# Modulation blocks laid out contiguous, a pinned order for the opening, and the convolution's taps split around the attention

## The chip, the cores and the metric

The kernel runs on one core of a Trainium2 chip: five engines with a queue each (TensorE or PE for matmuls, VectorE or DVE, ScalarE or ACT, GpSimd or POOL, SyncE or SP, which here only issues DMAs), an on-chip memory SBUF, and PSUM, into which TensorE writes. The metric is the device time of one execution in microseconds, as a median over runs.

## What is computed

One layer of a hybrid block on 512 tokens of width 1024, all in float32. Cut to what matters here:

```python
mod = silu(c) @ mod_w + mod_b                    # c: 1024 values; mod_w: 1024 x 6144
sh1, sc1, g1, sh2, sc2, g2 = split(mod, 6)
h = rms_norm(x, norm1_g) * (1 + sc1) + sh1       # x: 512 x 1024
proj = h @ w_in                                  # w_in: 1024 x 7680, split into ten parts
cv_a, cv_g, hg_q, hg_f, hg_i, hg_g, sb_q, sb_k, sb_v, gl = split(proj, ...)
u = causal_conv31(cv_a * sigmoid(cv_g)) + b      # 512 channels, 31 taps each
y_conv = silu(layer_norm(u)) @ w_conv            # branch 1
y_hgrn = gated_linear_recurrence(hg_q, hg_f, hg_i, hg_g) @ w_hgrn    # branch 2
y_sb = stick_breaking_attention(sb_q, sb_k, sb_v) @ w_sb             # branch 3, 8 heads
x = x + g1 * ((sig(gl0) * y_conv + sig(gl1) * y_hgrn + sig(gl2) * y_sb) @ w_out)
x = x + g2 * (relu(mod_norm(x) @ w1) ** 2 @ w2)
```

## The kernel before, in words

Activations lie transposed, 128 channels on the partitions and 512 tokens along the row. Each operand of a large matmul is split into a rounded part and the rest (`hilo`: ACT writes the rounded part at L83, DVE subtracts at L84), and each product is three matmuls (`mm3`, L113 to L115). Weights are loaded by SP in pieces of 1 MB (`cols_stage`, L329) and split in the order in which `add_cols` and `add_rows` list them, two pieces ahead of their use.

The program is written in one order, and a scheduler fixes each engine's own order from that and from its model of durations; an instruction that is ready may be taken ahead of earlier ones. An engine then runs its list strictly in that order. `tc.issue_after(i)` adds a rule: what is traced inside it stands behind instruction `i` on `i`'s engine. `high_priority` moves work ahead.

**Opening.** Small vectors (`vecs`) and the tap weights (`conv_w`) come on ACT's queue; x (four tiles), then the modulation block and the 768 weight columns of slab 0 on SP's. A modulation block (`load_ms`) is the part of `mod_w` that gives shift and scale for 128 channels: two DMAs of 512 KB in pieces of 512 B. PE first transposes vectors and tap weights (L170, L175), runs eight warm-up matmuls (L285), and then goes through eight slabs. For slab j: `prep_mod` multiplies the block by silu(c) into two accumulators, adds them on DVE (L241), and sums over partitions on PE with a vector of ones (L245); `prep_h` transposes x (L254), modulates (L258) and splits it; `prep_w` splits the slab's weights; `first_mm` makes 18 matmuls into six PSUM banks: two tiles of `cv_a` and the four of `cv_g`. Before slab 0, `x_norm` squares (ACT) and scales (DVE, L226) each x tile.

**After it.** Four tiles `k_in`, four `q_in` (24 matmuls each), the scans of `decay` (L616), `scores` (whose first product per head pair is `gram`, L650), the rows `hv_in` and `states`; then two more `cv_a` tiles (`conv_in`), eight `sb_in` tiles and `sv_in` for the attention; then four head pairs of attention, with a gate tile `hg_in` after each. A head's part of it is three score matmuls per row block, two sigmoids on ACT, a reversed running product and a product on DVE (L545, L546), transposes on PE (L557) and the product with v (L573).

**Taps.** The convolution is 31 DVE instructions for each of four channel tiles, `tap(i, d)`. The first of each is traced behind `head_norm`; the other 120 wait in a list and are traced within the branches at the end (`hook0`, `hook1`), with the attention ahead of them in program order. `conv_sum` and `conv_norm` follow them, and branch `cv`, the last of three, needs their result.

Of the kernel before, what the change touches and what calls it, by code (L numbers as in the profile page):

```python
# [15 lines left out]
P = 128  # L16
# [22 lines left out]
def tile_hybrid_block(ctx, tc, x, vecs, mod_w, mod_b, w_in, conv_w, w_conv, w_hgrn, w_sb, w_out, w1, w2, out):  # L39
# [42 lines left out]
    def hilo(src, hi, lo):  # L82
        A.activation(hi, src, AF.Copy)  # L83
        V.tensor_tensor(out=lo, in0=src, in1=hi.bitcast(F32), op=ALU.subtract)  # L84
# [25 lines left out]
    def mm3(o, lhs, rhs, start, stop):  # L110
        lh, ll = lhs
        rh, rl = rhs
        TE.matmul(o, lhsT=lh, rhs=rh, start=start, stop=False)  # L113
        TE.matmul(o, lhsT=lh, rhs=rl, start=False, stop=False)  # L114
        TE.matmul(o, lhsT=ll, rhs=rh, start=False, stop=stop)  # L115
# [3 lines left out]
    A.dma_start(vrow, vecs)  # L119
    cw_row = S((CW, 512), g="c0")  # L120
    A.dma_start(cw_row, conv_w)
# [13 lines left out]
    slabs = {}  # L135

    def load_slab(j):
        slabs[j] = wpool.tile([P, W0], F32, name="slab", bufs=10)
        SY.dma_start(slabs[j], wi_row[:, j, C_A + 256:C_A + 256 + W0])

    for t in range(NT):
        xt.append(P4((P, D), g="x0"))
        SY.dma_start(xt[t], x_v[t])
    load_ms(0)
# [28 lines left out]
    cp = ax()  # L173
    for i in range(4):
        TE.transpose(cp[:, i * 32:i * 32 + CW], cw_row[:, i * P:(i + 1) * P], ident[0:CW, 0:CW])  # L175
    cwc = C([P, 4, 32], F32)
    V.tensor_copy(cwc[:, :, 0:CW], cp[:, 0:128].rearrange("p (i k) -> p i k", k=32)[:, :, 0:CW])

# [18 lines left out]

    gbh = C([P, 24], F32)
    V.tensor_scalar(out=gbh, in0=vcol[:, V_GB:V_GB + 24], scalar1=0.5, scalar2=None, op0=ALU.mult)
    lnh = C([P, 8], F32)  # L200
    V.tensor_scalar(out=lnh, in0=vcol[:, V_LG:V_LG + 8], scalar1=0.5, scalar2=None, op0=ALU.mult)
# [9 lines left out]

    facc = [mm() if i < 4 else ps("f") for i in range(6)]
    hT, fw = [], {}
# [8 lines left out]
    def x_norm(t):  # L222
        junk = P4((P, D), g="x0")
        after(first, junk, xt[t], AF.Square, accum_out=stat[:, t:t + 1])
        rstd_small(stat[:, 4 + t:5 + t], stat[:, t:t + 1], D)
        V.tensor_scalar(out=xt[t], in0=xt[t], scalar1=stat[:, 4 + t:5 + t], scalar2=None, op0=ALU.mult)  # L226

    def prep_mod(j):
        ms = ms_t.pop(j)
        acc = S((P, 2, 2, P), g="acc")  # L230
        for kk in range(KT):
            a, src, c = acc[:, kk % 2], ms[:, :, kk, :], cact[:, kk:kk + 1]
            if kk < 2 and j == 0:
                V.tensor_scalar(out=a, in0=src, scalar1=c, scalar2=None, op0=ALU.mult)
            elif kk < 2:
                A.activation(a, src, AF.Identity, scale=c)
            else:
                V.scalar_tensor_tensor(out=a, in0=src, scalar=c, in1=a, op0=ALU.mult, op1=ALU.add)
        ne = 2 if j == 0 else 1
        if ne == 1:  # L240
            V.tensor_tensor(out=acc[:, 0], in0=acc[:, 0], in1=acc[:, 1], op=ALU.add)  # L241
        tp = ps("tp")
        for q in range(2):
            for e in range(ne):
                TE.matmul(tp[:, q:q + 1], lhsT=acc[:, e, q, :], rhs=ones[:, 0:1], start=(e == 0), stop=(e == ne - 1))  # L245
        gs, sh = modc[:, j:j + 1], modc[:, 8 + j:9 + j]
        V.scalar_tensor_tensor(out=gs, in0=tp[:, 0:1], scalar=mb1[:, j:j + 1], in1=vcol[:, V_N1 + j:V_N1 + j + 1], op0=ALU.add, op1=ALU.mult)
        V.tensor_tensor(out=sh, in0=tp[:, 1:2], in1=vcol[:, V_MB + j:V_MB + j + 1], op=ALU.add)

    def prep_h(j):  # L250
# [7 lines left out]
        b = A.activation(hf, tq, AF.Identity, scale=gs, bias=sh)  # L258
        if j == 3:
            ph.ops.append(b)  # L260
        hilo(hf, hh, hl)
        hT.append((hh, hl))

# [5 lines left out]
    def prep(j):  # L269
        load_ms(j)  # L270
        load_slab(j)
        prep_mod(j)
        prep_h(j)
        prep_w(j)

    def first_mm(j):
        wh, wl = fw.pop(j)
        for i in range(6):
            c = slice(i * P, (i + 1) * P)
            mm3(facc[i], (wh[:, c], wl[:, c]), hT[j], j == 0, j == KT - 1)  # L280
# [245 lines left out]

    LAY = {0: (0, 0), 1: (1, 0), 3: (1, 384), 2: (2, 0)}
    FILL = (512, 512, 256)

    def sb_weights(h):  # L530
# [3 lines left out]
        for tb in range(NT):  # L534
# [11 lines left out]
            V.tensor_tensor(out=bt[:, 0:n - 1], in0=bt[:, 0:n - 1], in1=kp[:, 1:n], op=ALU.mult)  # L546
# [249 lines left out]
    hnh = C([P, 1], F32)  # L796
    V.tensor_scalar(out=hnh, in0=vcol[:, V_HN:V_HN + 1], scalar1=0.5, scalar2=None, op0=ALU.mult)
# [16 lines left out]
    for i in range(2):  # L814
        conv_in(i, ch_tile("ca", i))
    for i in range(4):
# [98 lines left out]

    def hook0(j):
        run_bg(5, taps)
# [3 lines left out]
    def hook1(j):  # L921
        for d, f in ((0, lambda: (run_bg(len(taps), taps), conv_sum())), (1, conv_center), (2, conv_norm), (3, lambda: hls.append(parts(cacc)))):
# [123 lines left out]
def host_layout(inputs):  # L1046
# [31 lines left out]
```

## Time and profile before

| | |
|---|---|
| median of 3 runs | 922.64 us (922.06 to 924.39) |
| profiled execution, its own time | 924.09 us |
| its span, first to last instruction | 922.3 us |
| PE busy | 894.8 us, 97% of the span |
| DVE busy | 599.5 us, 65% |
| ACT busy | 385.8 us, 42% |
| moved by DMA | 107.78 MB, 117 GB/s on average |

Engines work side by side, so shares do not add up. An idle engine matters only where it is the one that the others wait for; over most of this span that is PE.

### The profile page before, as it was taken

The page shows a single profiled execution, that of the slowest core. Times are in us where ns is not written, and L with a number is a line of the kernel's source. Part 1 is how long each engine was busy: PE and PEld are TensorE (multiplying, and loading weights), DVE is VectorE, ACT ScalarE, POOL GpSimd, SP SyncE. Part 2 cuts the span into 40 slices and gives each one's busy share as a digit, 9 for nine tenths or more (in the row PEclk, how much of TensorE's full clock was granted, in tenths as well). Part 3 has the DMA queues.
Part 4 walks back from the last instruction along what each step waited for, and adds up shares of the span by engine and source line. Part 5 has one row for each costly group of instructions (what it writes and reads, how often), then busy time and mean ns, then how long its engine had stood idle before and what let it go on. Part 6 is the DMA issues. An engine that isn't in the chain of part 4 may idle for free.

```text
span 922.3 us, 10624 instructions
## 1 busy us (share of the span) xinstructions
PE 894.8 (97%) x4185; PEld 728.8 (79%) x4185; DVE 599.5 (65%) x886; ACT 385.8 (42%) x596; POOL 28.1 (3%) x35
## 2 busy tenths in 40 slices
PE   4999989999988999999999999999999999999998
PEld 2788878888755588888888888888888888888886
DVE  4882388899999999997965544774423254442422
ACT  4652434475788632223833536453312123431210
POOL 1002000001032000000000000000000000000000
PEclk9999999999999999999999999999999999999999
DMA  9981301131200344793423620552242233142121
GB/s 279 279 268 59 113 12 46 52 132 46 91 1 1 115 159 162 245 329 136 138 86 103 216 70 1 192 196 91 92 137 92 56 113 106 46 137 92 68 69 46
DMA packets 85418, 107.78 MB, mean 117 GB/s; under 512 B 2270, under 2 KB 58705, under 8 KB 85368
## 3 DMA queue, kind: packets, MB, share of 16 engines
q1 hardware_dynamic: 85200, 106.96, 35.5%
q8 instruction: 33, 0.54, 0.3%
q14 instruction: 17, 0.14, 0.1%
q10 hardware_dynamic: 168, 0.14, 0.0%
HBM read 105.00 MB, written 2.10 MB: 116 GB/s over the span
## 4 chain that ended last, share of the span: by engine, by line
PE 88%; DVE 6%; ACT 3%; DMA 2%; issue 1%; SPq 1%; DVEq 0%; ACTq 0%
PE mm L113 14%; PE mm L114 14%; PE mm L115 14%; PE ax L115 9%; PE ax L113 9%; PE ax L114 9%; PE o L115 2%; PE o L114 2%; PE o L113 2%; PE g L113 2%; PE g L114 2%; PE g L115 2%; PE g L654 1%; DVE bt L545 1%; PE o L573 1%; DVE bt L546 1%
## 5 line engine op out<-in xcount | busy, mean ns | idle before, releaser
L84 DVE TENSOR_TENSOR wl<-w,wh 128x1024 fp32r<-128x1024 f32 x134 | 162.8, 1221 | 194.4 <-ACT wh L83 147.4
L83 ACT ACTIVATE wh<-w 128x1024 fp32r<-128x1024 f32 x134 | 139.8, 1054 | 290.8 <-PE ax L115 129.9
L113 PE MATMUL mm<-ht,wh 128*128 128x512 f32 x272 | 106.7, 392 | 0.0
L115 PE MATMUL mm<-ht,wl 128*128 128x512 f32 x272 | 106.6, 392 | 0.0
L114 PE MATMUL mm<-ht,wh 128*128 128x512 f32 x272 | 106.6, 392 | 0.0
L114 PE MATMUL mm<-p,wh 128*128 128x512 f32 (+1 forms) x272 | 102.6, 378 | 0.0
L115 PE MATMUL mm<-p,wl 128*128 128x512 f32 (+1 forms) x272 | 102.4, 377 | 0.0
L113 PE MATMUL mm<-p,wh 128*128 128x512 f32 (+1 forms) x272 | 102.3, 377 | 0.0
L462 DVE SCALAR_TENSOR_TENSOR cv<-cv,cbig 128x511 f32<-128x511 f32 (+29 forms) x120 | 83.5, 733 | 0.0
L113 PEld LDWEIGHTS mm<-ht,wh 128*128 128x128 f32 x272 | 51.1, 188 | 11.2 <-issue 0.8
L114 PEld LDWEIGHTS mm<-ht,wh 128*128 128x128 f32 x272 | 51.1, 188 | 11.0 <-issue 0.6
L115 PEld LDWEIGHTS mm<-ht,wl 128*128 128x128 f32 x272 | 51.1, 188 | 10.4 <-issue 0.2
L114 PEld LDWEIGHTS mm<-p,wh 128*128 128x128 f32 x272 | 51.2, 188 | 9.4
L115 PEld LDWEIGHTS mm<-p,wl 128*128 128x128 f32 x272 | 51.2, 188 | 9.4
L113 PEld LDWEIGHTS mm<-p,wh 128*128 128x128 f32 x272 | 51.0, 188 | 9.3
L113 PE MATMUL ax<-wh,p 128*128 128x512 f32 x128 | 49.8, 389 | 0.0
L114 PE MATMUL ax<-wl,p 128*128 128x512 f32 x128 | 49.8, 389 | 0.0
L115 PE MATMUL ax<-wh,p 128*128 128x512 f32 x128 | 49.8, 389 | 0.0
L113 PE MATMUL ax<-wh,s 128*128 128x512 f32 x128 | 49.8, 389 | 0.0
L114 PE MATMUL ax<-wl,s 128*128 128x512 f32 x128 | 49.8, 389 | 0.0
L115 PE MATMUL ax<-wh,s 128*128 128x512 f32 x128 | 49.8, 389 | 0.0
L865 DVE SCALAR_TENSOR_TENSOR s<-p,cbig,s 128x512 f32<-128x512 f32 x64 | 47.1, 746 | 1.5 <-DMA p<-in_mod_w_dram 1.2
(248 smaller groups left out, 1666.8 us busy)
## 6 DMA issues: line engine op xcount, KB each, us to landing
w<-in_w_dram SPq DMA_DIRECT2D x32, 1024.0 KB, 5.7
w<-in_w_in_dram SPq DMA_DIRECT2D x27, 1024.0 KB, 5.3
p<-in_mod_w_dram SPq DMA_DIRECT2D x32, 512.0 KB, 7.4
ms<-in_mod_w_dram SPq DMA_DIRECT2D x16, 512.0 KB, 5.9
w<-in_w_out_dram SPq DMA_DIRECT2D x4, 1024.0 KB
slab<-in_w_in_dram SPq DMA_DIRECT2D x8, 384.0 KB, 4.6
x<-in_x_dram SPq DMA_DIRECT2D x4, 512.0 KB, 8.9
w<-in_w_hgrn_dram SPq DMA_DIRECT2D x2, 1024.0 KB, 4.9
```

What stands on the lines that cost most here:

```text
L83: A.activation(hi, src, AF.Copy)
L84: V.tensor_tensor(out=lo, in0=src, in1=hi.bitcast(F32), op=ALU.subtract)
L113: TE.matmul(o, lhsT=lh, rhs=rh, start=start, stop=False)
L114: TE.matmul(o, lhsT=lh, rhs=rl, start=False, stop=False)
L115: TE.matmul(o, lhsT=ll, rhs=rh, start=False, stop=stop)
L462: V.scalar_tensor_tensor(out=cacc[i][:, d:], in0=cu[i][:, 0:T - d], scalar=w, in1=cacc[i][:, d:], op0=ALU.mult, op1=ALU.add)
L545: V.tensor_tensor_scan(out=kp[:, 0:n][:, ::-1], data0=kp[:, 0:n][:, ::-1], data1=kp[:, 0:n][:, ::-1], initial=1.0, op0=ALU.mult, op1=ALU.b ...
L546: V.tensor_tensor(out=bt[:, 0:n - 1], in0=bt[:, 0:n - 1], in1=kp[:, 1:n], op=ALU.mult)
L573: TE.matmul(o[h * 64:h * 64 + 64, sb * P:T], lhsT=svt[sb][:, pr * P + h * 64:pr * P + h * 64 + 64], rhs=ahs[h][bi][:, off:off + n], start= ...
L654: TE.matmul(o[:, b * n:(b + 1) * n], lhsT=l, rhs=r, start=True, stop=True)
L865: V.scalar_tensor_tensor(out=a, in0=box["s"][:, kk, :], scalar=cact[:, 2 * k2 + kk:2 * k2 + kk + 1], in1=a, op0=ALU.mult, op1=ALU.add)
```

## The change

The first 2048 columns of `mod_w` are also laid out on the host as eight blocks in which each partition's 8 KB lie together, so `load_ms` is one DMA of 1 MB, with four buffers for three. x moves to ACT's queue, behind the vectors; the tap weights and the small columns for later stages (`lb_columns`, `conv_columns`) are traced inside the slab loop. Block 0 is summed wholly on PE (`prep_sum(0)`, 16 matmuls straight from the block), and for the other slabs PE sums the two accumulators itself (two matmuls more, no addition on DVE). Six warm-up matmuls stay of eight. In the loop, the work that prepares slab j stands behind the split of slab j-2, and its sums and transposes behind the first nine matmuls of slab j-1. The weights of later stages stand behind the last slab in SP's queue.

The two `cv_a` tiles come before the q tiles. Of the 120 taps, 24 are traced with the k tiles, 12 with the two `cv_a` tiles and 16 with the q tiles; the other 68 stand behind the last product of the attention on DVE. The diff, with returned handles, `lb_columns` and a few moved lines left out:

```diff
-    cw_row = S((CW, 512), g="c0")
-    A.dma_start(cw_row, conv_w)
...
     def load_ms(j):
-        ms_t[j] = wpool.tile([P, 2, 8, P], F32, name="ms", bufs=3)
-        for q in range(2):
-            c0 = (D if q == 0 else 0) + j * P
-            SY.dma_start(ms_t[j][:, q], mw_v[:, :, c0:c0 + P])
+        ms_t[j] = wpool.tile([P, 2, 8, P], F32, name="ms", bufs=4)
+        SY.dma_start(ms_t[j], mod_a[j])
...
+    load_ms(0)
     for t in range(NT):
         xt.append(P4((P, D), g="x0"))
-        SY.dma_start(xt[t], x_v[t])
-    load_ms(0)
+        with tc.issue_after(vdma.ins):
+            A.dma_start(xt[t], x_v[t])
     load_slab(0)
...
+    def conv_columns():
+        cw_row = S((CW, 512), g="c0")
+        with tc.issue_after(hb[3].ins):
+            A.dma_start(cw_row, conv_w)
+        cp = ax()
+        for i in range(4):
+            TE.transpose(cp[:, i * 32:i * 32 + CW], cw_row[:, i * P:(i + 1) * P], ident[0:CW, 0:CW])
...
-            if kk < 2 and j == 0:
-                V.tensor_scalar(out=a, in0=src, scalar1=c, scalar2=None, op0=ALU.mult)
-            elif kk < 2:
+            if kk < 2:
                 A.activation(a, src, AF.Identity, scale=c)
...
-        ne = 2 if j == 0 else 1
-        if ne == 1:
-            V.tensor_tensor(out=acc[:, 0], in0=acc[:, 0], in1=acc[:, 1], op=ALU.add)
+        return acc
+
+    def prep_sum(j, acc=None):
         tp = ps("tp")
+        ms = None if acc is not None else ms_t.pop(j)
         for q in range(2):
-            for e in range(ne):
-                TE.matmul(tp[:, q:q + 1], lhsT=acc[:, e, q, :], rhs=ones[:, 0:1], start=(e == 0), stop=(e == ne - 1))
+            if ms is not None:
+                for kk in range(KT):
+                    TE.matmul(tp[:, q:q + 1], lhsT=ms[:, q, kk, :], rhs=cact[:, kk:kk + 1], start=(kk == 0), stop=(kk == KT - 1))
+                continue
+            for e in range(2):
+                TE.matmul(tp[:, q:q + 1], lhsT=acc[:, e, q, :], rhs=ones[:, 0:1], start=(e == 0), stop=(e == 1))
...
-    for i in range(8):
+    for i in range(6):
         TE.matmul(wu, lhsT=ident, rhs=scanm.rearrange("p a t -> p (a t)"), start=True, stop=True)
+    prep_sum(0)
     for t in range(NT):
-        x_norm(t)
-    prep_mod(0)
-    prep_h(0)
-    prep_w(0)
+        last = x_norm(t)
+    with tc.issue_after(last[0].ins), tc.issue_after(last[1].ins):
+        prep_w(0)
+    ready = [prep_h(0)]
     for j in range(1, KT + 1):
         if j < KT:
-            prep(j)
-        first_mm(j - 1)
+            load_ms(j)
+            load_slab(j)
+            behind = ready[max(j - 2, 0)]
+            with tc.issue_after(behind[0].ins), tc.issue_after(behind[1].ins):
+                acc = prep_mod(j)
+                prep_w(j)
+        mid = first_mm(j - 1, range(3))
+        if j < KT:
+            with tc.issue_after(mid.ins):
+                prep_sum(j, acc)
+                ready.append(prep_h(j))
+        first_mm(j - 1, range(3, 6))
+        if j == 2:
+            lb_columns()
+        if j == 4:
+            conv_columns()
...
-        SY.dma_start(t, wv)
+        with tc.issue_after(last_load[0].ins):
+            SY.dma_start(t, wv)
...
     add_cols("hf", w_in, H_F, 4)
+    add_cols("ca", w_in, C_A, 2)
     add_cols("hq", w_in, H_Q, 4)
     add_rows("hi", w_in, H_I, 0, KT)
-    add_cols("ca", w_in, C_A, 2)
...
-            V.tensor_tensor(out=bt[:, 0:n - 1], in0=bt[:, 0:n - 1], in1=kp[:, 1:n], op=ALU.mult)
+            sb_last[:] = [V.tensor_tensor(out=bt[:, 0:n - 1], in0=bt[:, 0:n - 1], in1=kp[:, 1:n], op=ALU.mult)]
...
-    for h in range(4):
-        k_in(h)
+    for i in (2, 3):
+        tap(i, 0)
+    for j in range(1, CW):
+        for i in (2, 3):
+            bg.append(lambda i=i, j=j: tap(i, j))
+    with tc.issue_after(mid.ins):
+        for h in range(4):
+            k_in(h)
+            run_bg(6)
+    for i in range(2):
+        conv_in(i, ch_tile("ca", i))
+        tap(i, 0)
+        run_bg(6)
+    for j in range(1, CW):
+        for i in (0, 1):
+            bg.append(lambda i=i, j=j: tap(i, j))
     HP[0] = 2000
     for h in range(4):
         q_in(h)
+        run_bg(4)
...
-    for i in range(2):
-        conv_in(i, ch_tile("ca", i))
-    for i in range(4):
-        tap(i, 0)
-    for pr in ((2, 3), (0, 1)):
-        for j in range(1, CW):
-            for i in pr:
-                bg.append(lambda i=i, j=j: tap(i, j))
...
+    def late_taps(n):
+        with tc.issue_after(sb_last[0].ins):
+            run_bg(n, taps)
+
     def hook0(j):
-        run_bg(5, taps)
+        late_taps(5)
```

## Rows read from the trace of the kernel before

**Rows 1.** Busy time in stretches: PE, PEld, DVE, ACT, POOL; clock, DMA share, GB/s.

```profile
66.00:110.00 44.00, 44.00 (x196) 36.43 (x195) 13.23 (x18) 12.45 (x17) 5.55 (x2) 1.00 0.25 82
250.00:313.30 63.30, 57.44 (x297) 38.23 (x295) 62.25 (x102) 51.24 (x117) 12.38 (x8) 1.00 0.10 34
320.00:440.00 120.00, 120.00 (x546) 99.85 (x546) 110.76 (x160) 34.99 (x44) 1.06 (x2) 1.00 0.61 214
```

**Rows 2.** Timeline of the opening: start, duration, instruction, idle time before and releaser.

```profile
10.91 0.63 PE L175 MATMUL ax<-crs,c 31*128 31x31 f32 x4 [5.71 <-DMA c<-in_conv_w_dram]
11.47 8.56 PE L285 MATMUL tq<-cbig,crs 128*128 128x512 f32 x16
...
16.27 1.04 ACT L88 ACTIVATE x<-x 128x1024 f32<-128x1024 f32 x1
17.31 0.42 ACT L88 ACTIVATE cbig<-cbig 128x1 f32<-128x1 f32 x2
...
19.88 0.95 PE L245 MATMUL tp<-crs,acc 128*128 128x1 f32 x8
20.87 0.74 DVE L226 TENSOR_SCALAR x<-x,cbig 128x1024 f32<-128x1024 f32 x1
...
22.71 0.78 ACT L258 ACTIVATE s<-tq,cbig 128x512 f32<-128x512 f32 x1 [2.04 <-DVE cbig L248]
23.98 0.51 ACT L236 ACTIVATE acc<-ms,cbig 128x256 f32<-128x256 f32 x1 [0.49 <-DMA ms<-in_mod_w_dram]
24.40 0.61 ACT L83 ACTIVATE ht<-s 128x512 fp32r<-128x512 f32 x1
...
25.06 2.07 PE L113 MATMUL mm<-ht,fwh 128*128 128x512 f32 x4 [2.63 <-ACT ht L83]
...
65.79 0.39 PE L115 MATMUL f<-ht,fwl 128*128 128x512 f32 x1
```

**Rows 3.** Busy time in short stretches of the opening; the last two columns are DMA.

```profile
0.00:2.00 2.00, 0.00 (x0) 0.00 (x0) 0.00 (x0) 0.40 (x1) 1.47 (x8) 1.00 0.12 27
...
4.00:8.00 4.00, 0.42 (x1) 0.18 (x1) 0.28 (x1) 1.25 (x3) 0.44 (x3) 1.00 1.00 369
40.00:45.00 5.00, 5.00 (x27) 4.22 (x26) 4.66 (x13) 4.20 (x7) 0.00 (x0) 1.00 1.12 325
```

**Rows 4.** Timeline of PE: first and last of 48 matmuls, then the stop.

```profile
109.31 0.39 PE L113 MATMUL ax<-wh,ht 128*128 128x512 f32 x1
...
119.96 0.39 PE L115 MATMUL ax<-wh,ht 128*128 128x512 f32 x1
122.67 0.65 PE L650 MATMUL g<-tl 128*64 128x64 f32 x8 [2.32 <-DVE tl L677]
```

**Rows 5.** The chain of waits within the slabs: start, time on the chain, what.

```profile
32.90 0.39 PE tp L245 x4
...
36.38 0.44 PE tq L254 x4
```

**Rows 6.** Timeline of slab 2: start of its summing, rounding of its tile.

```profile
32.73 0.56 PE L245 MATMUL tp<-crs,acc 128*128 128x1 f32 x4
...
34.54 0.63 ACT L83 ACTIVATE ht<-s 128x512 fp32r<-128x512 f32 x1
```

**Rows 7.** Timeline of DVE: the scans, and seven taps in a row.

```profile
113.22 4.57 DVE L616 TENSOR_TENSOR_SCAN B<-cbig,B 128x512 f32<-128x512 f32 x4 [1.62 <-ACT B L88]
...
412.64 4.53 DVE L462 SCALAR_TENSOR_TENSOR cv<-cv,cbig 128x486 f32<-128x486 f32 x7
```

**Rows 8.** Busy time of the taps' line alone (DVE) in three stretches.

```profile
190.00:250.00 60.00, 29.31 (x42) 1.00 0.16 54
250.00:313.30 63.30, 6.55 (x9) 1.00 0.10 34
313.30:440.00 126.70, 47.65 (x70) 1.00 0.59 206
```

**Rows 9.** Groups of PE from 250 to 313.3 us: busy, mean; idle before, releasers.

```profile
L557 PE MATMUL tb<-crs,bt 128*128 128x128 f32 x73 | 14.6, 281 | 4.7 <-DVE bt L546 4.1 <-ACT wh L83 0.6
```

More of the change, by code (lines that the diff above doesn't have):

```diff
@@ L38, in tile_hybrid_block @@
 @with_exitstack
-def tile_hybrid_block(ctx, tc, x, vecs, mod_w, mod_b, w_in, conv_w, w_conv, w_hgrn, w_sb, w_out, w1, w2, out):
+def tile_hybrid_block(ctx, tc, x, vecs, mod_a, mod_w, mod_b, w_in, conv_w, w_conv, w_hgrn, w_sb, w_out, w1, w2, out):
     nc = tc.nc
@@ L82, in hilo @@
     def hilo(src, hi, lo):
-        A.activation(hi, src, AF.Copy)
-        V.tensor_tensor(out=lo, in0=src, in1=hi.bitcast(F32), op=ALU.subtract)
+        a = A.activation(hi, src, AF.Copy)
+        return a, V.tensor_tensor(out=lo, in0=src, in1=hi.bitcast(F32), op=ALU.subtract)
     def after(bi, *args, **kw):
@@ L114, in mm3 @@
         TE.matmul(o, lhsT=lh, rhs=rl, start=False, stop=False)
-        TE.matmul(o, lhsT=ll, rhs=rh, start=False, stop=stop)
+        return TE.matmul(o, lhsT=ll, rhs=rh, start=False, stop=stop)
     vrow = S((NVEC, P), g="c0")
-    A.dma_start(vrow, vecs)
-    cw_row = S((CW, 512), g="c0")
-    A.dma_start(cw_row, conv_w)
+    vdma = A.dma_start(vrow, vecs)
     x_v = x.rearrange("(a p) d -> a p d", p=P)
@@ L209, in tile_hybrid_block, with lb_columns @@
     modc = C([P, 16], F32)
+    cwc = C([P, 4, 32], F32)
+    oml = C([P, 4], F32)
+    gbh = C([P, 24], F32)
+    lnh = C([P, 8], F32)
+    hnh = C([P, 1], F32)
+    def conv_columns():
[5 more added lines that the diff above has]
+            TE.transpose(cp[:, i * 32:i * 32 + CW], cw_row[:, i * P:(i + 1) * P], ident[0:CW, 0:CW])
+        V.tensor_copy(cwc[:, :, 0:CW], cp[:, 0:128].rearrange("p (i k) -> p i k", k=32)[:, :, 0:CW])
+    def lb_columns():
+        lb = vcol[:, V_HLB:V_HLB + 4]
+        lbe = C([P, 4], F32)
+        lbs = C([P, 4], F32)
+        V.tensor_tensor(out=lbe, in0=lb, in1=lb, op=ALU.subtract)
+        ph(lbe, lbe, AF.Exp)
+        V.reciprocal(out=lbs, in_=lbe)
+        V.tensor_tensor(out=lbe, in0=lbe, in1=lbs, op=ALU.mult)
+        V.tensor_tensor(out=lbs, in0=lbe, in1=lbe, op=ALU.subtract)
+        V.tensor_scalar(out=oml, in0=lbs, scalar1=-1.0, scalar2=1.0, op0=ALU.mult, op1=ALU.add)
+        V.tensor_scalar(out=gbh, in0=vcol[:, V_GB:V_GB + 24], scalar1=0.5, scalar2=None, op0=ALU.mult)
+        V.tensor_scalar(out=lnh, in0=vcol[:, V_LG:V_LG + 8], scalar1=0.5, scalar2=None, op0=ALU.mult)
+        V.tensor_scalar(out=hnh, in0=vcol[:, V_HN:V_HN + 1], scalar1=0.5, scalar2=None, op0=ALU.mult)
     facc = [mm() if i < 4 else ps("f") for i in range(6)]
-    hT, fw = [], {}
+    hT, fw, hb = [], {}, []
     def rstd_small(dst, ssq, n):
@@ L225, in x_norm @@
         rstd_small(stat[:, 4 + t:5 + t], stat[:, t:t + 1], D)
-        V.tensor_scalar(out=xt[t], in0=xt[t], scalar1=stat[:, 4 + t:5 + t], scalar2=None, op0=ALU.mult)
+        b = V.tensor_scalar(out=xt[t], in0=xt[t], scalar1=stat[:, 4 + t:5 + t], scalar2=None, op0=ALU.mult)
+        return ph.ops[-1], b
     def prep_mod(j):
@@ L267, in prep_w, with first_mm @@
         fw[j] = (wh, wl)
[L269 to L278, printed above, removed]
+    def first_mm(j, tiles):
+        wh, wl = fw[j]
+        for i in tiles:
             c = slice(i * P, (i + 1) * P)
-            mm3(facc[i], (wh[:, c], wl[:, c]), hT[j], j == 0, j == KT - 1)
+            b = mm3(facc[i], (wh[:, c], wl[:, c]), hT[j], j == 0, j == KT - 1)
+        return b
     wu = ps("tq")
-    for i in range(8):
+    for i in range(6):
         TE.matmul(wu, lhsT=ident, rhs=scanm.rearrange("p a t -> p (a t)"), start=True, stop=True)
+    prep_sum(0)
     for t in range(NT):
-        x_norm(t)
-    prep_mod(0)
-    prep_h(0)
-    prep_w(0)
+        last = x_norm(t)
+    with tc.issue_after(last[0].ins), tc.issue_after(last[1].ins):
+        prep_w(0)
+    ready = [prep_h(0)]
     for j in range(1, KT + 1):
         if j < KT:
-            prep(j)
-        first_mm(j - 1)
+            load_ms(j)
[14 more added lines that the diff above has]
+            conv_columns()
     dij = S((P, P), I32, g="mk")
@@ L921, in hook1 @@
     def hook1(j):
-        for d, f in ((0, lambda: (run_bg(len(taps), taps), conv_sum())), (1, conv_center), (2, conv_norm), (3, lambda: hls.append(parts(cacc)))):
+        for d, f in ((0, lambda: (late_taps(len(taps)), conv_sum())), (1, conv_center), (2, conv_norm), (3, lambda: hls.append(parts(cacc)))):
             if j == 4 + d:
```

32 lines of the change are left out of this document (7 added, 25 removed).

## The prediction

> **What bounds the kernel now.** I read the busy times by stretch first, then the opening in order of time, then the chain of waits. From 320 us to 440 us TensorE (PE) is busy all the time, and so it is from 66 to 110 [rows 1]; the table above says 97% for the whole span. So the only time to win lies where PE waits or does work that nobody needs: the opening, one stop near 122 us, and the attention, where PE is busy for 57.4 of 63.3 us [rows 1]. The rest can only move as a block.
>
> In the opening the reader should see three late things [rows 2]. TensorE stands 5.71 us until 10.91, because the transposes of the tap weights wait for their own DMA; the warm-up matmuls stand in line behind them and end only at 20.0. The last x tile is scaled on VectorE (DVE) from 20.87 to 21.6. Then ScalarE (ACT) waits 0.49 us for a modulation block that a later slab needs, and works on it 0.5 us, ahead of the rounding that the first real matmul waits for. That matmul starts at 25.06, and the last of slab 7 at 65.79.
>
> **The opening after the change.** The tap weights leave the front, so the warm-up starts when the vectors are in, near 5.3 us. Sixteen records took 8.56 us [rows 2]; if the first four go at half the pace of the others, as 0.86 and 0.43 us, twelve take 6.9, until 12.2. Block 0 of the modulation is then summed on PE alone: 16 matmuls, two records each, where 8 records took 0.95 us [rows 2], so 3.8 us, until 16.0. Both end before the last x tile is normalised (below, 16.6), so I cost them at nothing; if the summing ran at half the clock it would end at 19.8 and the first matmul would slip by 3 us.
>
> The last x tile sets the start. Before, x had the DMA engines nearly to itself and moved at 369 GB/s from 4 to 8 us, with hardly a byte before 2.0 us [rows 3]. Now it goes out on ACT's queue while SP sends block 0, slab 0, block 1 and so on. x is 2.1 MB. Lower bound: x as if alone, 2.0 + 2.1/0.369 = 7.7 us. Upper bound: behind all that SP can issue before it waits for a buffer (four blocks of 1.05 MB and four slabs of 0.39 MB, 5.8 MB): 2.0 + 7.9/0.369 = 23.4. I take equal shares, 4.2 MB, 13.4 us, and my allowance of 0.8 for the last bytes and the signal: 14.2. Two queues that always have work, and no row that favours one, are the reason. From there by rows 2: square to the end of its two small activations 1.46 (16.27 to 17.73), scaling 0.74, one tile of transposes 0.3, modulating 0.78, rounding 0.61, and 0.3 of gaps: 4.2. First matmul at 18.4, 6.7 us earlier than before.
>
> The Trainium skill ("DMA: Bandwidth & Descriptors", section "Queues, rings and completion order") says that each DMA engine takes turns between the queues that have work for it, one packet at a time. A second queue then gives x no bandwidth of its own: by that rule x lands at 14.2 and the sum is as above, while a reader who took the ACT queue for a private road would get 8.5 and a first matmul near 13 as far as x decides. No row here has two busy queues at once, so this case's trace does not decide it yet.
>
> **What the slabs cost after that.** Back to back a 512-column matmul takes (119.96 - 109.31)/47 = 0.2266 us [rows 4], so 144 of them take 32.6. Before, each later slab added one set of transposes, 0.44, and one summing of four records, 0.39 [rows 5]: 7 x 0.83 = 5.8. From 25.06 to 66.02 are 40.96 us; with two early matmuls of the next stage (0.45) that leaves 2.1 us for the slow clock at the start. After, the accumulators are no longer added on DVE but on PE, so a summing has eight records, 0.78: 7 x 1.22 = 8.5. This is a price of 2.7 us on the bound engine.
>
> The pinned order puts the summing in the middle of a slab's 18 matmuls. From its end to the end of the rounding took 35.17 - 32.73 - 0.39 = 2.05 us [rows 6]; transposes and nine matmuls cover 0.44 + 2.04 = 2.48. So 0.4 us to spare, which one DVE or ACT instruction in the way can use up. I put 1.5 us of stalls on seven slabs, most of it at slab 1, whose sums may start only after slab 0 is split; the bounds are 0 and 5 (0.7 each). The transfers hold nothing up: in 8 KB rows I give the modulation blocks the 369 GB/s of x, against 325 for the old mix [rows 3]; 1.44 MB per slab takes 3.9 us against a pace of 5.3 on PE. All 13.6 MB up to the last slab are due near 40 us, so the weights queued behind it have over 15 us before the stage that needs them.
>
> End of the stage: 18.4 + 32.6 + 8.5 + 2.1 + 1.5 = 63.1, against 66.02 - 0.45 = 65.6 before. **Term 1: -2.5 us.** Ends: x as if alone and no stalls would give -9.7 by this sum, but the 32 summing records (until 16.0, then modulating and rounding: 18) hold it at -4.4; x behind everything gives +7.5.
>
> **Taps before the attention.** 52 of the 120 taps go into the stretch of the k, conv and q tiles (24 + 12 + 16). Seven taps took 4.53 us in a row [rows 7], 0.647 each: 33.6 us, and 2.2 for the four first taps. DVE was busy for 13.23 of 44 us there [rows 1], so 30.8 are free; the two conv tiles now moved in add 10.9 us of PE time and, at the same share, 7.6 free. 35.8 of work in 38.4 of room: it fits, at a cost of nothing, but with 2.6 us in hand. The conv tiles only change places with later tiles; PE has them to do either way. The stop of 2.32 us at 122.67, where the first gram waits for DVE [rows 4], stays: **term 2: 0**, from -2.3 to the rival below.
>
> **Taps in and after the attention.** Before, 29.3 us of taps ran from 190 to 250, 6.6 in the attention and 47.7 after it [rows 8]. The first were free, since PE was full. Without the 6.6, DVE has 62.25 - 6.55 = 55.7 us of its own there [rows 1] and PE 57.4: PE would be the bound, so 63.3 - 57.4 = 5.9 us is the most to win. The least is nothing: an idle PE may come from the order of short steps on three engines rather than from taps. Of the 4.7 us that PE idles before the transposes, 4.1 end with the product that DVE writes [rows 9], and taps stand in that queue; I take the middle. **Term 3: -3.0 us.** Afterwards 68 taps remain, 68 x 0.70 = 47.6 us, the same as the 47.7 that ran there before, so the convolution's end keeps its distance to the attention's end and PE stays full.
>
> **Sum.** -2.5 + 0 - 3.0 = -5.5. The profiled execution took 924.09 us with a span of 922.3; so a span near 916.8, and 918.6 for such an execution. The profiled one lies 1.45 above the median of 922.64, so the prediction for the median is 917.1. About 0.3% (2.8 us) is what a measurement of this kernel can tell from no change.
>
> **Rivals.**
> 1. *x comes late.* SP's blocks have rows twice as long as those of x; if the engines' turns are counted in rows, x gets a third: 6.3 MB, 2.0 + 17.1 + 0.8 = 19.9, first matmul at 24.1, stage end 68.8, +3.2 in place of -2.5. Total 922.64 + 3.2 - 3.0 = 922.8, no change. For it: x loses the head start that it had. Against: nothing in the trace weighs queues.
> 2. *Taps hold up the scans: slower.* The 16 taps of the q tiles stand in program order ahead of the scans that the grams need. DVE has 2.6 us in hand. If they all run late, the scans (which before waited 1.62 us for ACT, [rows 7]) start 16 x 0.647 - 1.6 = 8.7 us later, and PE, already stopped there, stops as much longer: 917.1 + 8.7 = 925.8. It decides from 5.5 us of lateness, which cancels the rest, and is a measurable loss from 8.3 on. For it: 0.70 us, a tap's full length, in place of 0.647 fills the room to the last microsecond. Against: tiles of q carry only four taps, so DVE catches up there.
> 3. *All of it comes.* First matmul at 18 without stalls (-4.4), PE full in the attention (-5.9), and half of the stop at 122 gone (-1.2): 911.1. For it: DVE's own work falls below PE's in the attention. Against: every one of the three must come.
> 4. *The opening gives nothing.* If slabs stall 0.7 us each, term 1 is +0.9 and only the attention is left: 920.5.
>
> **Chances.** The forecast (-5.5, its own range 914 to 920) 0.42; rival 1 0.13; rival 2 0.15; rival 3 0.20; rival 4 0.10. The forecast gives 0.37 faster and 0.05 same; rival 3 0.20 faster; rival 4 0.04 faster and 0.06 same; rival 1 0.08 same, 0.05 slower; rival 2 0.03 same, 0.12 slower. Together 0.61 faster, 0.22 same, 0.17 slower. The range, 910 to 925, leaves out the later half of rival 2 and a third of rival 3, together 0.14.
>
> **What would show it.** The first real matmul between 17 and 20 us (24 would be rival 1); the last of slab 7 near 63; tap instructions from 64 us on with DVE over 85% busy until 118; the wait before the first gram at 2 to 3 us (8 or more is rival 2); no tap between sv's end and the last product of the attention, and PE idle there by about 3 us in place of 5.9; PE full from then on. The prediction fails most easily through an order on PE or DVE that differs from program order: an engine that stands behind one instruction that is late.

## The result, and the profile after

The changed kernel takes 930.84 us (median of 4 runs, 929.32 to 932.26) against 922.38 for the kernel before (4 runs): a ratio of 1.0087, with a 95% interval from 1.0061 to 1.0113. It is 8.5 us slower, where 917.1 was predicted; it lies outside the range, and on the side that was given 17 in 100. The profiled execution took 932.15 us with a span of 930.4.

The opening first. The timeline of the kernel after: TensorE (PE), then ScalarE (ACT) with the four x tiles.

```profile
7.64 0.43 PE L167 MATMUL ax<-crs,c 115*128 115x115 f32 x1 [7.64 <-DMA c<-in_vecs_dram]
7.86 7.51 PE L290 MATMUL tq<-cbig,crs 128*128 128x512 f32 x12
15.21 3.63 PE L252 MATMUL tp<-cbig,ms 128*128 128x1 f32 x32
...
21.44 0.47 PE L264 MATMUL tq<-crs,x 128*128 128x128 f32 x1 [2.32 <-DVE x L232]
...
24.71 2.07 PE L113 MATMUL mm<-ht,fwh 128*128 128x512 f32 x4 [2.13 <-ACT ht L83]
...
74.14 0.39 PE L115 MATMUL f<-ht,fwl 128*128 128x512 f32 x1
```

```profile
10.36 1.06 ACT L88 ACTIVATE x<-x 128x1024 f32<-128x1024 f32 x1 [1.73 <-DMA x<-in_x_dram]
...
13.34 1.06 ACT L88 ACTIVATE x<-x 128x1024 f32<-128x1024 f32 x1 [1.45 <-DMA x<-in_x_dram]
...
16.34 1.06 ACT L88 ACTIVATE x<-x 128x1024 f32<-128x1024 f32 x1 [1.52 <-DMA x<-in_x_dram]
...
19.35 1.06 ACT L88 ACTIVATE x<-x 128x1024 f32<-128x1024 f32 x1 [1.54 <-DMA x<-in_x_dram]
```

The reader should see that ACT waits for the DMA before each of the four tiles, and that they come 3.0 us apart. PE's warm-up does start earlier, at 7.86 in place of 11.47 [rows 2], and the sums of block 0 take 3.63 us, near the 3.8 worked out; but the last x tile is there only at 19.35, so the first real matmul comes at 24.71, 0.35 us earlier than before [rows 2] and not 6.7. The last matmul of slab 7 ends at 74.37 (the next starts there), against 66.02 before. From there to the end of the span are 856.0 us, and 856.7 before, counted from 65.6. So the loss lies in the eight slabs: 49.7 us from the first matmul to the end, where 40.5 were needed before.

What PE waited for in the first 75 us of the kernel after, besides the vectors (us in total, times, longest):

```profile
PE mm L113 <- ACT ht L83: 4.0, 6, 2.1
PE tq L264 <- DVE x L232: 2.5, 2, 2.3
PE ax L198 <- DMA c<-in_conv_w_dram: 1.1, 1, 1.1
```

And the stretches of the opening (the column ahead of the last two is PE's granted clock, as a share of 2.4 GHz):

```profile
4.00:8.00 4.00, 0.36 (x2) 0.39 (x3) 0.00 (x0) 0.72 (x1) 0.44 (x3) 1.00 1.00 411
10.00:15.00 5.00, 5.00 (x10) 2.06 (x9) 1.06 (x5) 3.02 (x8) 0.00 (x0) 1.00 1.02 414
15.00:20.00 5.00, 4.12 (x35) 3.66 (x33) 1.12 (x2) 2.12 (x5) 0.00 (x0) 0.91 1.02 413
20.00:25.00 5.00, 1.24 (x3) 0.65 (x4) 2.79 (x6) 3.51 (x10) 0.00 (x0) 0.50 1.02 381
25.00:30.00 5.00, 5.00 (x17) 3.93 (x17) 3.63 (x8) 2.72 (x6) 0.00 (x0) 0.57 0.54 164
```

The bytes are not the trouble: 405 to 414 GB/s move from 4 to 20 us, more than the 369 of before [rows 3]. But the clock is at half, 1.2 GHz, from about 19 us (0.91 is the mean from 15 to 20) until nearly 30 us: slab 0's matmuls run at half pace. It falls right behind the one-column sums of block 0, which end at 18.84, and PE's thin stretch (1.24 us busy from 20 to 25) comes after the fall.

I cut the stage into parts by the starts on PE's timeline: a matmul's pace of 0.2266 us; what each transpose and sum takes; how much later than the pace a matmul starts where the row names a releaser (waits); and the excess of matmuls that run at over 0.33 us each (slow clock). The last column is the twelfth experiment below.

| us | before | predicted | after | twelfth |
|---|---|---|---|---|
| first real matmul | 25.1 | 18.4 | 24.7 | 18.7 |
| 144 matmuls, small gaps | 33.6 | 32.6 | 33.8 | 33.9 |
| slow clock | 1.4 | 2.1 | 3.1 | 3.3 |
| sums | 3.0 | 5.4 | 5.6 | 2.7 |
| transposes | 2.6 | 3.1 | 2.9 | 2.9 |
| waits (for h and conv_w) | 0 | 1.5 | 4.0 | 0.4 |
| transposes of conv_w | - | - | 0.3 | - |
| end of slab 7 | 65.6 | 63.1 | 74.4 | 61.9 |

Then the other terms. The stop before the first gram, groups of the attention from 250 to 320 us (PE, VectorE or DVE, ScalarE or ACT) and its busy times, and the taps' line alone, all of the kernel after but for the first line of the third block, which is of the kernel before from 250 to 313.3 us:

```profile
142.26 0.98 PE L672 MATMUL g<-tl 128*64 128x64 f32 x7 [2.33 <-DVE tl L699]
```

```profile
L579 PE MATMUL tb<-crs,bt 128*128 128x128 f32 x63 | 12.5, 281 | 4.8 <-DVE bt L568 3.5 <-DVE hg L659 1.2
```

```profile
L545 DVE TENSOR_TENSOR_SCAN bt<-bt 128x128 f32<-128x128 f32 (+3 forms) x32 | 25.6, 824 | 0.4 <-ACT bt L88 0.3
...
L567 DVE TENSOR_TENSOR_SCAN bt<-bt 128x128 f32<-128x128 f32 (+3 forms) x29 | 22.7, 812 | 3.9 <-ACT bt L88 3.8
...
L88 ACT ACTIVATE bt<-z 128x128 f32<-128x128 f32 (+3 forms) x59 | 21.9, 430 | 3.6 <-DVE bt L568 2.8 <-PE z L563 0.6
```

```profile
250.00:320.00 70.00, 64.72 (x329) 44.83 (x329) 59.06 (x93) 59.49 (x127) 12.55 (x8) 1.00 0.09 31
```

```profile
66.00:125.00 59.00, 34.03 (x50) 1.00 0.31 103
...
250.00:330.00 80.00, 2.67 (x4) 1.00 0.21 71
330.00:460.00 130.00, 44.14 (x65) 1.00 0.50 175
```

The stop is where it was and as long (2.33 against 2.32 us, [rows 4]). The taps ran where they were meant to: 50 of them by 125 us, none in the attention (the four counted up to 330 us start at 326.29, behind its last product), 65 after that. PE still stands 5.3 us of the 70 in the attention, and 4.8 of it before the same transposes as before [rows 9]. What changed is one step further back: DVE, freed from taps, now waits 3.9 us ahead of its scans, 3.8 of them for ACT's sigmoids, and ACT in turn waits 2.8 us ahead of these for the product on DVE.

### The profile page after: what moved, and what is told of

Read it like the earlier page. It is cut to its first block, busy times and chain, and to the rows that moved or that the text cites. A ratio compares the mean times of both kernels' runs of the same rounds, so it can differ in the third digit from the quotient of the medians.

```text
span 930.4 us, 10711 instructions
## 1 busy us (share of the span) xinstructions
PE 902.2 (97%) x4233; PEld 733.6 (79%) x4233; DVE 597.9 (64%) x871; ACT 387.5 (42%) x596; POOL 34.8 (4%) x35
## 4 chain that ended last, share of the span: by engine, by line
PE 87%; DVE 5%; ACT 3%; DMA 3%; issue 1%; ACTq 0%; DVEq 0%
PE mm L113 14%; PE mm L114 13%; PE mm L115 13%; PE ax L113 9%; PE ax L115 9%; PE ax L114 9%; PE o L114 2%; PE o L113 2%; PE o L115 2%; DVE bt L567 2%; PE g L113 2%; DMA x<-in_x_dram 2%; PE g L115 2%; PE g L114 2%; PE g L676 1%
```

## The experiments

My theory after the profile: the whole loss is in the opening; x is late because ACT's queue gets less than half of the bandwidth behind the vectors' small rows; and the slabs are slow because h is late on PE, in part through the sums. The rivals are named with each run. Ratios are to the kernel before.

**1. The opening alone.** The new layout, queues and pins; `ca` and the taps as before.

```
 add_cols("hf", w_in, H_F, 4)
-add_cols("ca", w_in, C_A, 2)
 add_cols("hq", w_in, H_Q, 4)
 add_rows("hi", w_in, H_I, 0, KT)
+add_cols("ca", w_in, C_A, 2)
...
-            run_bg(6)
...
-        late_taps(5)
+        run_bg(5, taps)
```

> The opening of the changed kernel with the tap order and the place of the two conv tiles as before. Theory: the whole loss is in the opening, where slab 7 ends at 74.4 us in place of 65.6 (8.8 us), and the rest gives back 0.7. Then this kernel takes 8 to 9 us more than the one before, about 931, and PE's idle time in the attention stays near 6 us. Rival: the taps in the early stretch cost something too, or the opening only looks late because it was pinned with them; then it stays under 927.

931.31 us (930.38 to 932.61), 1.0097 [1.0082, 1.0112]. All of the loss is here.

**2. The taps alone.** The kernel before with `ca` and the taps as in the change.

> The opening of the kernel before, with the conv tiles moved and the taps split around the attention. Theory (loss is all in the opening, taps were not what PE waited for in the attention): within 1.5 us of the kernel before, 921 to 924, with PE idle 5 to 6 us in the attention although no tap stands there. Rival (taps are worth what the prediction's term 3 said): 3 us faster, 919 to 920. Second rival (taps hold up the scans): 925 or more, and a longer stop before the first gram.

922.05 us (10 runs), 0.9999 [0.9987, 1.0011]. Its busy times, to be read beside [rows 1]:

```profile
66.00:110.00 44.00, 44.00 (x196) 36.44 (x195) 43.78 (x66) 11.44 (x15) 12.84 (x2) 1.00 0.24 79
250.00:320.00 70.00, 64.21 (x329) 42.22 (x328) 63.38 (x104) 56.26 (x124) 13.02 (x9) 1.00 0.18 63
```

DVE is full from 66 to 110 (43.78 of 44) and PE none the worse for it: the early taps cost nothing. They bring nothing either: PE still stands 5.8 us in the attention.

**3. Vectors in 128 rows.** Padded from 115.

```
-    vrow = S((NVEC, P), g="c0")
+    vrow = S((P, P), g="c0")
```

> The changed kernel with the vectors padded from 115 to 128 rows, nothing else. Theory: DMA engines take turns between the two queues row by row; the 115 rows go to only a few engines, where each 512 B row waits for a row of 8 KB from SP, so the vectors land at 7.6 us and x stands behind them. With 128 rows on all engines the vectors land near 5 us, the first x tile near 7 in place of 10.4, the last near 16 in place of 19.4, the first real matmul near 21.5 in place of 24.7, and the time falls by 2 to 4 us. Rival: x is slow because SP has most of the bandwidth whatever stands before it; then the vectors land earlier but the last x tile still comes after 18.5 and the time falls by less than 1 us.

929.9 us (929.12 to 931.19), 1.0082 [1.0067, 1.0097]: 0.9 us less than after, with ranges that overlap, and not the 2 to 4 of the theory. The vectors are there at 6.21 in place of 7.64, the last x tile at 18.16 in place of 19.35. The small rows account for about 1.2 us of x's lateness; the rest has another cause.

**4. x first, on SP's queue,** ahead of block 0, as before the change.

```
+        SY.dma_start(xt[t], x_v[t])
+    load_ms(0)
-            A.dma_start(xt[t], x_v[t])
```

> The changed kernel with x on SP's queue ahead of block 0, as it was before; all else as changed. Theory (sharing the DMA engines with SP's blocks is what made x late): the last x tile is in by 10 us and squared by 12.5, so the sums of block 0 (which now lands later, near 13) and the warm-up decide: first real matmul at 17 to 19 in place of 24.7, time 5 to 7 us less than the changed kernel. Rival (the start is held by something else, such as the order on ScalarE or the vectors): the first matmul stays after 22 and the gain is under 2 us.

924.93 us (10 runs), 1.0034 [1.0021, 1.0047]: 5.9 us less than after. The last tile is squared at 11.33, the first real matmul comes at 18.44. So the order of the loads costs 6 us. That the prediction had 18.4 too is chance: there x decides, landing at 14.2, while here x is there 2.9 us earlier and PE's own line holds the start, the warm-up until 12.62 and then the sums of block 0:

```profile
12.62 3.63 PE L251 MATMUL tp<-cbig,ms 128*128 128x1 f32 x32
16.11 0.64 PE L263 MATMUL tq<-crs,x 128*128 128x128 f32 x4
18.44 2.08 PE L113 MATMUL mm<-ht,fwh 128*128 128x512 f32 x4 [1.69 <-ACT ht L83]
```

It is still slower than before, although it starts 6.6 us earlier: the slabs give that back. Its profiled execution lies 4.1 us above its median; in it PE waits 3.8 us for the rounding of h and, inside slab 4, 2.0 us for conv_w.

**5. The fourth, with conv_w loaded at the start,** right behind the vectors on ACT's queue.

> x first on SP as in the run before, and besides the tap weights' DMA issued at the start again, behind the vectors; their transposes stay inside slab 4. Theory: in the changed kernel that DMA is issued near 44 us, takes over 7 us beside the weights and is then waited for by PE inside a slab, and by the DVE copy behind which the next block's sums stand; with it early the wait is gone, slabs 4 and 5 fall to 5.9 us and below, and the time falls by 2 to 4 us against x first alone, to 921 to 923. Rival: the slabs are slow from something else (order, DVE), and the time stays within 1 us of 924.9.

925.72 us (925.44 to 926.44), 1.0041 [1.0027, 1.0055]: no gain on the fourth. The last x tile, in this kernel and then in the fourth:

```profile
14.02 1.06 ACT L88 ACTIVATE x<-x 128x1024 f32<-128x1024 f32 x1 [2.76 <-DMA x<-in_x_dram]
```

```profile
11.33 1.06 ACT L88 ACTIVATE x<-x 128x1024 f32<-128x1024 f32 x1 [1.33 <-DMA x<-in_x_dram]
```

62 KB of taps hold up x by 2.7 us, where 413 GB/s would carry 62 KB in 0.15. PE no longer waits for conv_w, but the first real matmul comes at 21.11: what was won at slab 4 was lost at the start. The Trainium skill ("DMA: Bandwidth & Descriptors", section "Why a DMA increments its semaphore by 16 and not by 1") says that a DMA started by SP or ACT uses as many of the 16 engines as the largest number up to 16 that divides its rows; by that rule 31 rows all go over one engine and 115 over five. One engine's share of the 413 is 25.8 GB/s, and 62 KB over it take 2.5 us, an estimate that the 2.7 agrees with.

**6. The fourth, with the two accumulators added on DVE** (so that a sum is four records on PE, as before).

```
+        V.tensor_tensor(out=acc[:, 0], in0=acc[:, 0], in1=acc[:, 1], op=ALU.add)
-            for e in range(2):
-                TE.matmul(tp[:, q:q + 1], lhsT=acc[:, e, q, :], ...
+            TE.matmul(tp[:, q:q + 1], lhsT=acc[:, 0, q, :], ..., start=True, stop=True)
```

> x first on SP, and the two accumulators of slabs 1 to 7 added on DVE again, so PE has four records fewer in each. Theory: PE is what the slabs wait for, so seven times 0.39 us, 2.7 us, come back: 922 to 923. Rival: the chain from the sums over the modulation to the rounding is what a slab waits for; then the added DVE step takes back what PE saves and the time stays within 1 us of 924.9.

922.72 us (10 runs), 1.0016 [1.0006, 1.0027]: 2.2 us less than the fourth, as the theory had it. On PE's timeline the sums take 2.5 us in place of the 5.6 of after. The stage ends at 65.95, so a start that is 6.5 us earlier than before is still all given back: PE waits 5.2 us in six places for the rounding of h, 1.7 of it ahead of slab 0.

**7. The changed kernel with each modulation block in two DMAs,** whose rows are then 4 KB, as long as those of x.

> The changed kernel with each modulation block in two DMAs of 4 KB rows, the length of x's rows, in place of one of 8 KB; same bytes, same queue, same order. Theory (the DMA engines' turns between the two queues are counted in rows or packets of a row, not in bytes): x's share grows, the vectors land by 5.5 us in place of 7.6, the last x tile by 17 in place of 19.4, first real matmul at 22 to 23, time 1 to 3 us less. Rival (the share goes by bytes or by how full a queue is): vectors and x land as before within 0.7 us.

928.87 us (927.24 to 929.71), 1.0072 [1.0054, 1.0091], 2 us less than after. The vectors come at 5.23 (after: 7.64), and the x tiles are squared at 8.64, 11.21, 13.77 and 16.18, 2.51 us apart: 0.524 MB in 2.51 us are 209 GB/s, half of the 410 that moved then. In the changed kernel they were 3.0 us apart: 175 of 413, 0.42. What the two queues moved, SP's (q1) and ACT's (q10), in packets, MB and share of the engines' time, in the kernel after from 8 to 18 us and then in this one from 6 to 15:

```profile
q1 hardware_dynamic: 511, 2.35, 57.8%
q10 hardware_dynamic: 502, 1.81, 45.2%
```

```profile
q10 hardware_dynamic: 520, 1.90, 52.2%
q1 hardware_dynamic: 526, 1.85, 50.6%
```

A packet here is a row, but for about one in eight, a signal of 4 bytes. Both queues get through as many rows, whatever their length, so the rival, shares by bytes, is out. In the kernel after SP's rows are 8 KB long for a block and 3 KB for a slab, 5.5 on average, so rows of 4 KB get 4 of 9.5, 0.42. Here they are 4, 4 and 3 KB, and x gets 4 of 7.7, 0.52 (measured 0.51). Whether a turn is one row or several, these counts do not tell. By the Trainium skill ("DMA: Bandwidth & Descriptors", section "Queues, rings and completion order"), as the prediction cites it, the queues take turns one packet at a time. The trace agrees as far as both queues move as many packets.

**8. Three mends at once:** the fifth and the sixth, with the activation table loaded behind the last h, not the fourth.

> x first, tap weights early, accumulators added on DVE, and the ScalarE table load that stands between modulating and rounding of slab 3 moved behind slab 7. Theory: the gains add up (about 3, 2.7 and 1 us below x first alone): 917 to 919.5, which beats the kernel before by 3 us or more. Rival: once one is mended another wait takes its place, and the time stays above 921.

928.36 us (927.59 to 929.22), 1.0069 [1.0053, 1.0086], 5.6 us more than the sixth: the theory failed. conv_w put off the start as in the fifth (first matmul 20.72, against 18.55). The table load only changed its slab, from one in the middle to the last, where nothing covers it. ACT in this kernel:

```profile
63.56 0.78 ACT L266 ACTIVATE s<-tq,cbig 128x512 f32<-128x512 f32 x1 [3.65 <-PE tq L262]
64.36 1.28 ACT L100 ACT_TABLE_LOAD   x1
65.66 0.63 ACT L83 ACTIVATE ht<-s 128x512 fp32r<-128x512 f32 x1
```

It stands between modulating and rounding, and PE starts slab 7 late by 1.48 us.

**9. The sixth, with two idle matmuls of 512 columns on PE** behind slab 0's transposes.

> Base: x first on SP's queue, accumulators added on DVE (922.72 us; first real matmul 18.55, slab 0 takes 9.79 us, granted clock 0.67 from 15 to 20 us and 0.64 from 20 to 25). Here two matmuls of 512 columns (1.28 us each in the opening) that compute nothing needed are put on PE behind the transposes of slab 0, in the 1.7 us that PE otherwise waits for the first block of h. Theory (the slow clock is a share of what the slabs cost, and it falls because PE does little ahead of slab 0): the granted clock stays near 1.00 from 17 to 23 us, the first real matmul comes about 1 us later at 19.4, slab 0 takes 6.5 us in place of 9.8, and the whole takes 920.5 us. Rival (the one-column matmuls before it have already brought the clock down, or the h of slab 1 is late by itself): slab 0 still takes over 9 us and the whole 923.5 us.

923.4 us, but its ten runs lie between 920.78 and 925.72, 1.0018 [1.0000, 1.0036]: no gain shown, and no loss that is one. Stretches of this kernel:

```profile
16.00:18.00 2.00, 2.00 (x13) 1.58 (x13) 0.82 (x3) 0.67 (x1) 0.00 (x0) 0.88 0.78 254
18.00:20.00 2.00, 2.00 (x4) 0.67 (x2) 1.20 (x3) 1.97 (x5) 0.00 (x0) 0.50 0.80 311
20.00:25.00 5.00, 5.00 (x25) 4.09 (x23) 3.47 (x8) 1.10 (x3) 0.00 (x0) 0.90 0.89 341
25.00:30.00 5.00, 2.82 (x9) 2.14 (x10) 4.64 (x12) 3.56 (x6) 0.00 (x0) 0.78 0.66 238
```

The clock is better at slab 0 (0.90 from 20 to 25), but both halves of the rival came. The clock falls before slab 0 all the same, at about 17.5, although PE, with the idle matmuls, is shown busy without a gap from 8 to 24 us: what stands ahead of it are the 32 one-column records of block 0's sums (13.12 to 16.75) and four transposes. And PE then waits 2.18 us for h of slab 1 (2.82 us busy from 25 to 30), and the half clock comes back there: slabs 0 and 1 together take 15.58 us, against 15.26 in the sixth. No run with x first sums block 0 on DVE again, so what these sums cost in clock stays open.

**10. The sixth, without the pins of the slab loop.**

```
-            with tc.issue_after(behind[0].ins), tc.issue_after(behind[1].ins):
-                acc = prep_mod(j)
-                prep_w(j)
+            acc = prep_mod(j)
+            prep_w(j)
...
-            with tc.issue_after(mid.ins):
-                prep_sum(j, acc)
-                ready.append(prep_h(j))
+            prep_sum(j, acc)
+            ready.append(prep_h(j))
```

> The same base (922.72 us); the pins of the slab loop are taken out, both those that hold the modulation and the split of slab j behind the h of slab j-2 and those that hold its sum and transposes behind the middle of slab j-1, so that the scheduler's own order stands, as in the kernel before. Theory (the pins make h late: its modulating and rounding get only the nine matmuls behind the middle as cover, and each slab then starts with a wait of 0.2 to 2.2 us): the waits for the hi part of h at slab starts, 5.4 us in sum in the base, fall under 2.5 us, and the whole takes 920 us. Rival (what DVE and ACT have to do per slab sets it, whatever the order): the waits stay in sum and the whole is within 1 us of 922.7.

924.48 us (924.4 to 926.7), 1.0039 [1.0024, 1.0054]: 1.8 us more than the sixth, so the time went against the theory. Its mechanism did not. All of PE's waits from 14 to 70 us:

```profile
PE ax L197 <- DMA c<-in_conv_w_dram: 4.1, 1, 4.1
PE mm L113 <- ACT ht L83: 0.7, 1, 0.7
```

The wait for h falls from 5.2 to 0.7 us. But the slabs now run ahead of conv_w, whose DMA leaves ACT only behind the fourth h, and its transposes stand ahead of slab 4 on PE.

**11. The layout alone.** The kernel before with contiguous modulation blocks, one DMA each.

> The kernel before with one part of the change alone: each modulation block laid out contiguous and loaded by one DMA with rows of 8 KB in place of two with rows of 512 B; orders, queues and sums as before. Theory (the opening before is held by x, which lands ahead of block 0 on the same queue, and by DVE's eight passes over block 0; faster blocks only shorten the wait for block 0): block 0 lands about 1 us earlier, the first real matmul at 24.3 in place of 25.1, the whole 921.5 us. Rival (blocks are what the slabs wait for): the stage ends 3 us earlier, 919 us. Third: nothing, 922.2 us, since DVE's passes set the start.

920.97 us (10 runs) against 922.21, 0.9994 [0.9984, 1.0003]: not told from no change. The first real matmul comes at 23.75 and the clock is 1.00 in each stretch from 10 to 40 us; the stage ends at 62.8, in an execution of 920.87 us (before: 65.6, in one of 924.09).

**12. The tenth, with conv_w's transposes behind the middle of the last slab.**

```
-        if j == 4:
-            conv_columns()
+    with tc.issue_after(mid.ins):
+        conv_columns()
```

> Base: x first on SP's queue, accumulators added on DVE, no pins in the slab loop (924.48 us, in its profile 4.09 us of waiting on PE for conv_w ahead of slab 4, whose DMA leaves ACT only behind the fourth block of h). Here the four transposes of conv_w are held on PE behind the middle of the last slab, so that nothing of the stage waits for that DMA; it lands long before the taps need it. Theory (without the pins the slabs hardly wait any more, and what hid that was the one wait for conv_w): the stage ends 3.5 to 4 us earlier, at 63, and the whole takes 920.6 us, below the kernel before (922.2 us). Rival (PE's wait was cover for DVE and ACT, which are as far behind without it: the h of the next slabs become late instead): the stage ends at 66, the whole takes 924 us.

917.88 us (917.71 to 920.14), 0.9954 [0.9940, 0.9968] to the kernel before (922.32): it beats both kernels, by 4.4 and 13 us. PE's waits from 14 to 76 us, and the end of its stage:

```profile
PE mm L113 <- ACT ht L83: 1.0, 1, 1.0
PE mm L114 <- DVE ht L84: 0.2, 1, 0.2
```

```profile
18.69 2.07 PE L113 MATMUL mm<-ht,fwh 128*128 128x512 f32 x4 [0.99 <-ACT ht L83]
...
61.65 0.39 PE L115 MATMUL f<-ht,fwl 128*128 128x512 f32 x1
```

The stage ends at 61.9, in an execution of 920.14 us; the rival, that PE's wait was cover for DVE and ACT, is out.

## Why the prediction was wrong

**Term 1, the start (predicted 18.4, measured 24.71).** The step that failed is "I take equal shares, 4.2 MB, 13.4 us": x was to move at half of 369 GB/s from 2.0 us on and to land at 14.2; it landed at 19.35. The larger part is the start and not the share. x stands behind the vectors on ACT's queue, which the prediction's sum leaves out, and up to 5.5 us that queue had moved nothing but vectors:

```profile
q10 hardware_dynamic: 97, 0.05, 3.0%
```

Four tiles at 3.0 us each, taken back from 19.35 less the 0.8 for the signal, start at 6.5 us, 4.5 later than taken. The share was 0.42 and not 0.5, but of 413 GB/s and not of 369, so the four tiles took 12.0 us in place of 11.4, only 0.6 more. The seventh run separates the two: its last tile is 3.2 us earlier, 2.0 through the share and 1.2 through the start. Equal turns give each queue as many rows and not as many bytes; the prediction took the two for the same. Rival 1 had this mechanism, but that its numbers (19.9 and 24.1) came so near is chance: it has a third from 2.0 us on, and measured is 0.42 from 6.5. What holds x back until then is open: padding the vectors gave 1.2 us of it, but in the seventh run all their rows are through by 4.7 us and x's first row still starts only at 5.1, although its DMAs were issued from 1.34 us on.

From x's landing to the first matmul the prediction has 4.2 us; it took 5.36. DVE scales two tiles at once, and then splits slab 0's weights ahead of the two columns that the modulating on ACT waits for:

```profile
21.96 0.95 DVE L84 TENSOR_TENSOR fwl<-slab,fwh 128x768 fp32r<-128x768 f32 x1
...
23.22 0.78 ACT L268 ACTIVATE s<-tq,cbig 128x512 f32<-128x512 f32 x1 [1.42 <-DVE cbig L258]
```

Block 0 summed on PE costs nothing where x is late, as taken (it ends at 18.84). With x first it does: there the warm-up and these sums hold the first matmul at 18.44, near the 18 that the prediction names as this bound.

**Term 1, the slabs (predicted 44.7 us, measured 49.7).** By the table the sums and the transposes were sized right (8.4 against 8.5). The waits were not: 4.0 in place of 1.5, within the bounds of 0 to 5; 1.2 of them are for conv_w, below. The step "0.4 us to spare, which one DVE or ACT instruction in the way can use up" was true and should have been priced with what stands in the way. In the kernel after, two cases on ACT:

```profile
55.78 0.78 ACT L268 ACTIVATE s<-tq,cbig 128x512 f32<-128x512 f32 x1 [1.75 <-PE tq L264]
56.45 1.05 ACT L83 ACTIVATE wh<-w 128x1024 fp32r<-128x1024 f32 x1
57.40 0.62 ACT L83 ACTIVATE ht<-s 128x512 fp32r<-128x512 f32 x1
```

```profile
42.18 0.78 ACT L268 ACTIVATE s<-tq,cbig 128x512 f32<-128x512 f32 x1 [2.25 <-PE tq L264]
42.98 1.28 ACT L100 ACT_TABLE_LOAD   x1
44.27 0.63 ACT L83 ACTIVATE ht<-s 128x512 fp32r<-128x512 f32 x1
```

A split of the next stage's weights and the load of an activation table stand between modulating and rounding, and PE then waits 0.30 and 0.78 us. I had asked of these weights only whether they come in time, not what their early splits hold up. With the pins gone the waits are 0.4 us in sum. That pins, not work, make them is shown by runs 6, 10 and 12 together: work and loads are the same in them. Without the pins eight tile transposes stand ahead of slab 0 on PE in place of four: in the first slabs they run a slab earlier, and only the sum, modulating and rounding are left on the way. The matmuls themselves took 2.2 us more than the 34.7 taken with the slow clock: 1.2 in small gaps, which the kernel before had as well (33.6 in place of 32.6), and 1.0 in slow clock, which the fill of the ninth run did not bring back. conv_w's 7.5 us from its issue at 44.28 to PE's start on it at 51.76, where the prediction says that "the tap weights leave the front" and asks no more, cost PE 1.1 us and hid a gain in the tenth run. [rows 2] had a sign of it: before, too, these 62 KB on ACT's queue were there only at 10.91.

**What adds up.** From 930.84: x first -5.9, sums on DVE -2.2, pins out and conv_w late -4.8, to 917.88. The last two changes were only tried on top of the first; what the pins cost by themselves in the changed kernel was not run.

**Term 2 (0): right.** 2.33 us against 2.32. Rival 2, taps that hold up the scans, didn't come.

**Term 3 (-3.0): failed.** The changed kernel wins 0.7 us behind the stage at most, and the taps alone nothing (second run). Over the same 63.3 us of work, 8.8 us later, PE stands 5.3 us in place of 5.9. "The least is nothing: an idle PE may come from the order of short steps on three engines" is what happened. The step that failed is "taps stand in that queue; I take the middle", a price for the taps out of 4.1 us of waiting. DVE's queue was relieved and PE's idle time stayed: DVE's scans now wait for ACT (3.9 us, before 0.4), and ACT for DVE's product (2.8 us, before 1.8). That an engine is named as the releaser does not say that its load is the cause. That the two, by waiting for each other, set the pace is read from these rows; no run tried it.

## What to carry to other kernels

A transfer moved to a second queue gets no bandwidth of its own: write down what stands ahead of it on that queue and how long all the rows are that it takes turns with. When a forecast comes out, check that what it says decides is what decided: 18.44 against 18.4 was two other terms. An order pinned by hand fixes the slack as well; count what the other engines may slip in between, and run the kernel once without the pins, with the next wait in line moved out of the way, before judging either. A mend that shows nothing may have been eaten by the wait behind it: the tenth run lost time, and with one more edit it was the fastest.

## What the runs showed of the hardware

A DMA of 31 rows takes long beside heavy traffic: 62 KB took 7.5 us from issue to use in the kernel after, and issued early it put off x by 2.7 us. In rows of 3 to 8 KB the opening's loads moved at 405 to 414 GB/s from 4 to 20 us. Two busy queues got through as many rows in the same time (502 and 511, 520 and 526), so the bytes follow the rows' lengths: 0.42 for rows of 4 KB beside 5.5 on average, 0.51 beside 3.7. An idle PE is not all that stands ahead of a half clock. In each profile with block 0 summed on PE the clock falls during these 32 one-column records or within 1 us behind them; in the ninth run it was 0.50 from 18 to 20 us with PE shown busy in all of 8 to 24. The kernel before, with 8 such records, keeps 1.00 through them, and its clock first falls in a wait of 2.63 us (0.66 from 24 to 26).
